# Moving half of an output block behind the last input products, and folding the last rows in two parts

## The chip, the core and the metric

The kernel runs on one core of one Trainium2 chip. The metric is the device time of one execution in microseconds (us); a comparison uses the median of several runs. TensorE (PE) does the matmuls, VectorE (DVE) and ScalarE (ACT) the elementwise work, GpSimd (POOL) and SyncE (SP) issue transfers here.

## What is computed

A backbone of two layers over 512 latent tokens of width 1024 and 256 context tokens. Layer 0 is a bidirectional retention mixer; layer 1, whose end the change concerns, is a chunked gMLP without context output:

```python
u = h @ w_in[:, :GM_WIDTH]                       # GM_WIDTH = 2048
v = (h @ w_in[:, GM_WIDTH:2 * GM_WIDTH])
z = h @ w_in[:, 2 * GM_WIDTH:]
...                                              # v is normalised
mixed = einsum('gij,bnjgc->bnigc', w_s, vg) + b_s
y = u * mixed
out = (y * silu(z)) @ w_out                      # 2048 -> 1024
x = x + gate_x * out
return rmsnorm(x, final_g)
```

All of it is float32. The kernel forms each float32 matmul as three matmuls on a high and a low half of both operands.

## The kernel before

**Operands.** `mm3` issues the three matmuls of a product. A weight block comes as a raw float32 tile of 128 x 1024, in two transfers of 256 KB; ScalarE casts it to the high half (a cast `hl<-raw`), and VectorE subtracts that from the raw to give the low half (`hl<-raw,hl`). The pairs lie in a ring of `HL = 4` tiles.

**Products.** A large product is done by Winograd's form of 2 x 2 blocks with seven block products instead of eight. A quad is the seven: B11, T1, T2, B21, T3, B22, T4 (`SINGLE`), each of 24 matmuls of 256 columns. The T blocks are differences of raw blocks, formed in place on VectorE (`raw<-raw`), so that a quad keeps its four raw tiles until T3, B22 and T4 have been split. ScalarE copies three of the banks out (`snap`), and VectorE adds three of them to other banks (`snap<-pst,snap`).

**The end of layer 1.** The loop `for i in range(UZ)` has eight quads (`UZ = 8`). Quad i gives u and z of two feature tiles, 2i and 2i + 1, for all 512 tokens. After B22 the mixing matmuls on v are issued (16 of 128 columns), then the gating `gate_f` of feature 2i + 1, then T4, then `gate_f` of 2i. `gate_f` runs on ScalarE and VectorE and splits the gated feature (`ya`) into the high and low half for the output product. The features lie in six places `ys[f % 6]`: four in `hc`, two in the tags `g2` and `g3` (`yb`).

After quads 2, 4 and 6 `out1(p)` multiplies four features (4p to 4p + 3) by `w_out`, for p = 0, 1, 2; `out1(3)` follows quad 7. A block p has two halves `hf` of 512 output columns, each with two weight tiles and, for each of four token tiles t, four features k: 12 matmuls of 512 columns into one PSUM bank. `out1(3)` takes in its first half the features k = 0, 1, 3 of all four token tiles first and k = 2 of all four after that. `drain` adds a bank to the running sum `o1[t]`; for p = 2 it also multiplies by the gate and adds the residual (`xs`, loaded from `x1_d`). For p = 3 `final` squares the row half with its sum on ScalarE, multiplies by the final weight, and, after the second half, scales the row: columns 0 to 511 on VectorE and 512 to 1023 on ScalarE, each stored by a transfer of its own.

**Order.** TensorE's queue is kept in the order of the text through the class `Queue`. Those of VectorE, ScalarE and SP are, in this part of the kernel, settled by a scheduler when the kernel is built. Each engine then works its queue in order. `Stream` (`Q`) holds the weight blocks in the order in which they are used and their loads in the same order. It has seven raw slots `w0` to `w6`; a load is issued by SP once a slot is free, that is, once its last block has been split. The blocks of `out1(3)` are multiplied by the layer's gate on VectorE before they are split (`raw<-raw,gateb`). `Q.get()` splits two blocks ahead of the one that it hands out. `add_out(p)` puts the four blocks of an output block into the list, at the place where `out1(p)` stands in the loop. PSUM has six banks for these products and two (`tm`) for other sums.

All calls on the engines go through line 54, so that the profile's lines say L54 and the groups are told by their tiles.

Of the kernel before, what the change touches and what calls it, by code (L numbers as in the profile page):

```python
# [8 lines left out]
F32R = mybir.dt.float32r  # L9
AF = mybir.ActivationFunctionType  # L10
ALU = mybir.AluOpType
AX = mybir.AxisListType

P = 128
D = 1024
KT = D // P
SEQ = 512
CTX = 256
HEADS = 4
NT = SEQ // P  # L20
# [6 lines left out]
HS = 256  # L27
# [40 lines left out]
def hybrid_kernel(ctx, tc, xT_d, cT_d, cv_d, sv_d, rows_d, ada0_d, adag_d, w_d, rope_d, dec_d, ws_d, id_d, out_d):  # L68
    nc = tc.nc
    pe, act, dve, sp = (Queue(tc, e) for e in (nc.tensor, nc.scalar, nc.vector, nc.sync))  # L70
# [11 lines left out]
    def st(shape, tag, dt=F32, bufs=1, name=None):  # L82
        return sb.tile(shape, dt, tag=tag, name=name or tag, bufs=bufs)

    T2 = 11
# [32 lines left out]
    def t2(name, shape=(P, 512), dt=F32):  # L118
        return st(list(shape), "t2", dt, bufs=T2, name=name)

    def pt(shape=(P, 512), tag="ps"):
        return ps.tile(list(shape), F32, tag=tag, name="pst", bufs=6 if tag == "ps" else 2)
# [3 lines left out]
    def mm3(out, l, r, first, last):  # L126
        (lh, ll), (rh, rl) = l, r
        mm(out, ll, rh, start=first, stop=False, skip_group_check=True)
        mm(out, lh, rl, start=False, stop=False, skip_group_check=True)
        mm(out, lh, rh, start=False, stop=last, skip_group_check=True)  # L130
# [13 lines left out]
    def load(dst, src):  # L144
        sp.dma_start(dst, src)
# [95 lines left out]
    def parts_of(q, u):  # L241
        kind, i = q[0], q[1]
        kh, nh = int(u[0]) - 1, int(u[1]) - 1
        if kind == "kq":
            b = 16 * i + (0 if nh else 2)
            return narrow_parts(b, b + 1, kh)
        if kind == "vz":
            return wide_parts(16 * i + (8 if nh else 4), kh, q[2])
        if kind == "v1":
            return wide_parts(64 + 4 * i, kh, nh)  # L250
        return narrow_parts(80 + 2 * i + nh, 96 + 2 * i + nh, kh)
# [30 lines left out]
            for cb in (a, b):  # L282
                Q.load((("v1", cb), u), V1_SLOTS, 2, parts_of(("v1", cb), u))

    def add_out(p):
        for j in range(4):
            q = ("o", 4 * p + j)
            h = j // 2 * 512
            Q.single(q, ("gated", h) if p == 3 else "plain")
            Q.load((q, "w"), W, 2, [(lambda r, e=e: r[:, 512 * e:512 * e + 512], w_d[112 + 4 * p + 2 * (j % 2) + e][:, h:h + 512])  # L290
                                    for e in range(2)])

    UZ = 8
    for i in range(UZ):
        Q.quad(("u", i), SINGLE)
        for u in RAWS:
            Q.load((("u", i), u), W, 2, parts_of(("u", i), u))
        if i and i % 2 == 0:
            add_out(i // 2 - 1)
    add_out(3)  # L300


# [269 lines left out]
    def project(q):  # L572
        if q[0] == "kq":
            return Product(features, kq_done(q[1]), hc)
        return Product(tokens, vz_done(q[1], q[2]), hc)
# [349 lines left out]
    for n, q in enumerate(QUADS[3:]):  # L925
        pr = project(q)
# [287 lines left out]
    fg = st([P, D], "g0", name="fg")  # L1214
# [9 lines left out]
    o1 = [st([P, D], f"s{t}", name="o1") for t in range(NT)]  # L1224
    ya = st([P, 4, 2, SEQ], "hc", F32R, name="ya")
    ys = [ya[:, i] for i in range(4)] + [st([P, 2, SEQ], f"g{i}", F32R, name="yb") for i in (2, 3)]

    def yf(f):
        return ys[f % 6]

    def out1(p):
        for hf in range(2):
            ws = [Q.get() for _ in range(2)]
            pr = {}
            if p == 3 and hf == 0:
                seq = [(t, k) for ks in ((0, 1, 3), (2,)) for t in range(NT) for k in ks]
            else:
                seq = [(t, k) for t in range(NT) for k in range(4)]
            ends = (2,) if p == 3 and hf == 0 else (3,)
            for t, k in seq:  # L1240
                if k == 0:
                    pr[t] = pt()
                y = yf(4 * p + k)
                w = ws[k // 2][:, :, k % 2 * 512:k % 2 * 512 + 512]
                mm3(pr[t], (y[:, 0, t * P:t * P + P], y[:, 1, t * P:t * P + P]), (w[:, 0, :], w[:, 1, :]), k == 0, k in ends)
                if k in ends:
                    drain(p, t, hf, pr.pop(t))

    def drain(p, t, hf, pr):
        h = slice(hf * 512, hf * 512 + 512)  # L1250
        s = o1[t][:, h]
        if p == 0:
            act.copy(s, pr)
            return
        dve.tensor_tensor(s, pr, s, ALU.add)
        if p == 2:
            xs = t2("xs")
            load(xs, x1_d[2 * t + hf])
            dve.tensor_tensor(s, s, Q.gate[:, h], ALU.mult)
            dve.tensor_tensor(s, s, xs, ALU.add)  # L1260
        if p == 3:
            final(t, hf, s, h)

    ends = {}

    def final(t, hf, s, h):
        if hf == 0:
            ends[t] = (st([P, 2], "fss", bufs=4), st([P, D], f"w{t}", name="o"))
        ss, o = ends[t]
        act.activation(t2("junk1"), s, AF.Square, accum_out=ss[:, hf:hf + 1])  # L1270
        if hf == 0:
            dve.tensor_scalar(ss[:, 0:1], ss[:, 0:1], 1.0 / D, EPS, ALU.mult, ALU.add)
        dve.tensor_tensor(o[:, h], s, fg[:, h], ALU.mult)
        if hf == 0:
            return
        rows = out_d[t * P:t * P + P, :]
        act.activation(ss[:, 1:2], ss[:, 1:2], AF.Sqrt, bias=ss[:, 0:1], scale=1.0 / D)
        dve.reciprocal(ss[:, 1:2], ss[:, 1:2])
        dve.tensor_scalar(o[:, 0:512], o[:, 0:512], ss[:, 1:2], None, ALU.mult)
        load(rows[:, 0:512], o[:, 0:512])  # L1280
        act.activation(o[:, 512:], o[:, 512:], AF.Copy, scale=ss[:, 1:2])
        load(rows[:, 512:], o[:, 512:])

    vts = {}

    def load_vt(i):
        vts[i] = []
        for th in range(2):
            v = t2("vt", (P, 2, HS))
            load(v, vt_d[i][:, 2 * th:2 * th + 2, :])  # L1290
            for t in range(2):
                n = 2 * th + t
                dve.tensor_scalar(v[:, t, :], v[:, t, :], mv[:, n, 0:1], rv[:, n:n + 1], ALU.subtract, ALU.mult)
            vts[i].append(v)

    def gate_f(f, pm, mine):

        g = f // 2
        a = t2("ya")
        z1 = t2("yz")  # L1300
        bb = bsb[:, g * P:g * P + P].unsqueeze(1).to_broadcast([P, NT, P])
        for th in range(2):
            act.activation(z1[:, th * HS:th * HS + HS], mine[th][:, HS:], AF.Silu)
        dve.scalar_tensor_tensor(a.rearrange("p (n i) -> p n i", n=NT), pm.rearrange("p (n i) -> p n i", n=NT),
                                 vg[:, f:f + 1], bb, ALU.mult, ALU.add)
        for th in range(2):
            h = a[:, th * HS:th * HS + HS]
            dve.tensor_tensor(h, mine[th][:, 0:HS], h, ALU.mult)
        dve.tensor_tensor(a, a, z1, ALU.mult)
        y = yf(f)  # L1310
        split((y[:, 0, :], y[:, 1, :]), a)

    load_vt(0)
    for i in range(UZ):
        got, pms = {}, {}
        prod = Product(features, got.__setitem__)
        for name in SINGLE:
            prod.run(name, Q.get())
            if name == "T2" and i < UZ - 1:
                load_vt(i + 1)  # L1320
            if name == "B22":
                for s in range(2):
                    pm = pms[s] = pt()
                    for n in range(NT):
                        mm(pm[:, n * P:n * P + P], vts[i][n // 2][:, n % 2, s * P:s * P + P], wsT[:, i * P:i * P + P], start=True, stop=True)
                gate_f(2 * i + 1, pms[1], {0: got["12"], 1: got["22"]})
        gate_f(2 * i, pms[0], {0: got["11"], 1: got["21"]})
        if i and i % 2 == 0:
            out1(i // 2 - 1)
    out1(3)  # L1330


# [108 lines left out]
```

## Time and profile before

| What | Value |
|---|---|
| Time, median of 3 runs | 906.26 us |
| The three runs | 908.04, 906.09, 906.26 us |
| Profiled execution: span from first to last instruction | 908.2 us |
| Profiled execution: its own time | not given apart from the span |
| Mean granted TensorE clock | 0.992 |
| VectorE's busy time | 720.0 us (79%) |
| Chain that ended last | PE 67%, DVE 19%, DMA 5%, ACT 4%, issue 4% |

The span is that of one execution, which isn't necessarily one of the three timed ones. A busy share is an average over stages. Times in the timeline are microseconds from the start of the span, and each row has its start, its duration, engine, operation, the tiles written and read, the count, and in brackets the idle time before it with what ended it. The granted clock is the share of TensorE's full speed that the throttle allowed in a window.

### The profile page before, as it was taken

The page shows a single profiled execution, that of the slowest core. Times are in us where ns is not written, and L with a number is a line of the kernel's source. Part 1 is how long each engine was busy: PE and PEld are TensorE (multiplying, and loading weights), DVE is VectorE, ACT ScalarE, POOL GpSimd, SP SyncE. Part 2 cuts the span into 40 slices and gives each one's busy share as a digit, 9 for nine tenths or more (in the row PEclk, how much of TensorE's full clock was granted, in tenths as well). Part 3 has the DMA queues.
Part 4 walks back from the last instruction along what each step waited for, and adds up shares of the span by engine and source line. Part 5 has one row for each costly group of instructions (what it writes and reads, how often), then busy time and mean ns, then how long its engine had stood idle before and what let it go on. Part 6 is the DMA issues. An engine that isn't in the chain of part 4 may idle for free.

```text
span 908.2 us, 16915 instructions
## 1 busy us (share of the span) xinstructions
PE 884.4 (97%) x6872; PEld 839.3 (92%) x6872; DVE 720.0 (79%) x1024; ACT 445.8 (49%) x683; POOL 51.4 (6%) x88
## 2 busy tenths in 40 slices
PE   8999999999999999999999999999999999999986
PEld 7899999999999999998989898999999899899875
DVE  3689967698689876888677669999899478689975
ACT  5564634434445435626263558654445444353334
POOL 0001201101101011000000001111000000000000
PEclk9999999999999999999999999999999999999999
DMA  9933957467477458758253611636335035128002
GB/s 338 399 121 109 320 194 255 153 191 223 154 237 239 140 183 316 255 161 260 79 184 118 209 47 59 215 96 211 118 117 187 24 116 187 44 96 283 19 24 93
DMA packets 76782, 153.81 MB, mean 169 GB/s; under 512 B 7840, under 2 KB 34592, under 8 KB 76704
## 3 DMA queue, kind: packets, MB, share of 16 engines
q1 hardware_dynamic: 69840, 130.70, 44.2%
q0 software_dynamic: 6720, 22.03, 6.4%
q8 instruction: 54, 0.88, 0.4%
q14 instruction: 24, 0.20, 0.1%
q10 hardware_dynamic: 144, 0.01, 0.0%
HBM read 128.58 MB, written 24.12 MB: 168 GB/s over the span
## 4 chain that ended last, share of the span: by engine, by line
PE 67%; DVE 19%; DMA 5%; ACT 4%; issue 4%; SPq 1%; DVEq 0%; ACTq 0%
PE pst L54 67%; DVE hl L54 6%; DMA raw<-in_w_dram 3%; DVE raw L54 3%; DVE ya L54 2%; DVE o L54 2%; DVE snap L54 1%; SPq L54 1%; DMA vt<-vt 1%; DMA xq<-in_xT_dram 1%; ACT hl L54 1%; DVE f L54 1%; DVE pf L54 1%; ACT junk L54 1%; DVE oS L54 1%
## 5 line engine op out<-in xcount | busy, mean ns | idle before, releaser
L54 DVE TENSOR_TENSOR hl<-raw,hl 128x1024 fp32r<-128x1024 f32 x195 | 236.0, 1219 | 68.0 <-ACT hl L54 67.8
L54 ACT CAST hl<-raw 128x1024 fp32r<-128x1024 f32 x195 | 203.7, 1050 | 129.0 <-PE pst L54 71.2
L54 PE MATMUL pst<-oS,hl 128*128 128x256 f32 x1104 | 135.6, 282 | 4.6 <-DVE hl L54 3.9
L54 PE MATMUL pst<-hl,oS 128*128 128x256 f32 x1152 | 137.8, 281 | 2.0 <-DVE hl L54 1.8
L54 PEld LDWEIGHTS pst<-hl,oS 128*128 128x128 f32 x1152 | 135.8, 190 | 3.5 <-DVE hl L54 2.3
L54 PEld LDWEIGHTS pst<-oS,hl 128*128 128x128 f32 x1104 | 131.4, 190 | 6.9 <-ACT ya L54 3.7
L54 PE MATMUL pst<-oA,hl 128*128 128x256 f32 x936 | 117.5, 281 | 0.7 <-DVE snap L54 0.5
L54 PEld LDWEIGHTS pst<-oA,hl 128*128 128x128 f32 x936 | 112.2, 189 | 3.2 <-issue 1.3
L54 DVE TENSOR_TENSOR raw<-raw 128x1024 f32<-128x1024 f32 x92 | 111.4, 1218 | 1.2 <-DMA raw<-in_w_dram 0.5
L54 ACT COPY snap<-pst 128x512 f32<-128x512 f32 x92 | 53.9, 586 | 103.4 <-PE pst L54 102.9
L54 PE MATMUL pst<-hl,oA 128*128 128x256 f32 x816 | 98.6, 279 | 0.4 <-DVE snap L54 0.4
L54 PEld LDWEIGHTS pst<-hl,oA 128*128 128x128 f32 x816 | 96.3, 189 | 0.6 <-issue 0.6
L54 PE MATMUL pst<-og,hl 128*128 128x256 f32 x768 | 92.5, 281 | 0.0
L54 PEld LDWEIGHTS pst<-og,hl 128*128 128x128 f32 x768 | 90.4, 189 | 0.9 <-DVE acc L54 0.2
L54 PE MATMUL pst<-hl,ya 128*128 128x512 f32 x288 | 70.8, 399 | 2.7 <-DVE ya L54 2.7
L54 PEld LDWEIGHTS pst<-hl,ya 128*128 128x128 f32 x288 | 54.9, 192 | 15.2 <-DVE ya L54 3.1
L54 PE MATMUL pst<-v,ph 128*128 128x512 f32 x192 | 60.1, 395 | 0.0
L54 DVE TENSOR_TENSOR snap<-pst,snap 128x512 f32<-128x512 f32 x69 | 47.2, 684 | 3.9 <-PE pst L54 3.6
L54 ACT CAST ph<-pf 128x512 fp32r<-128x512 f32 x24 | 14.9, 621 | 67.1 <-DVE pf L54 66.7
L54 PE MATMUL pst<-hl,hc 128*128 128x256 f32 x384 | 47.4, 280 | 0.0
L54 PEld LDWEIGHTS pst<-hl,hc 128*128 128x128 f32 x384 | 46.0, 189 | 0.0
L54 PEld LDWEIGHTS pst<-v,ph 128*128 128x128 f32 x192 | 36.2, 188 | 7.3
(171 smaller groups left out, 970.3 us busy)
## 6 DMA issues: line engine op xcount, KB each, us to landing
raw<-in_w_dram SPq DMA_DIRECT2D x224, 256.0 KB, 4.4
bg<-in_adag_dram SPq DMA_DIRECT2D x32, 512.0 KB, 4.3
ada_w<-in_ada_dram SPq DMA_DIRECT2D x16, 512.0 KB, 8.7
raw<-in_w_dram SPq DMA_DIRECT2D x16, 512.0 KB, 4.3
bg<-in_dec_dram SPq DMA_DIRECT2D x12, 512.0 KB, 4.4
v<-snap POOLq DMA_DIRECT2D x16, 256.0 KB, 5.0
z<-snap POOLq DMA_DIRECT2D x16, 256.0 KB, 4.2
v<-v SPq DMA_DIRECT2D x8, 512.0 KB, 4.3
```

The source lines that it names most:

```text
L54: made = op(*args, **kw)
```

## The change

Block 2 of the output product is taken apart: its first half stays behind quad 6, its second half comes behind quad 7, ahead of `out1(3)`. The list of the blocks and loads follows. The features of quad 7 (14 and 15) get places of their own, in the tag `oA11`, whose operand is last read by quad 7's B11; before, they lay in two of the six places. The special order of the first half of `out1(3)` is dropped: each token tile takes its features 0 to 3 in turn. The last token tile's second half is done in two parts of 256 columns, each with a bank of its own, by `last_part`: the first part is added, squared and multiplied by the final weight while the second is in the matmuls; the row is then scaled with columns 0 to 767 on VectorE and 768 to 1023 on ScalarE, and stored by one transfer of 512 KB.

```diff
-    def add_out(p):
-        for j in range(4):
+    def add_out(p, js=range(4)):
+        for j in js:
...
         if i and i % 2 == 0:
-            add_out(i // 2 - 1)
+            add_out(i // 2 - 1, range(4 if i < UZ - 2 else 2))
+    add_out(2, (2, 3))
     add_out(3)
...
+    late_y = []
+
     def yf(f):
-        return ys[f % 6]
+        return ys[f % 6] if f < 14 else late_y[f - 14]
 
-    def out1(p):
-        for hf in range(2):
+    def out1(p, hfs=range(2)):
+        for hf in hfs:
             ws = [Q.get() for _ in range(2)]
-            pr = {}
-            if p == 3 and hf == 0:
-                seq = [(t, k) for ks in ((0, 1, 3), (2,)) for t in range(NT) for k in ks]
-            else:
-                seq = [(t, k) for t in range(NT) for k in range(4)]
-            ends = (2,) if p == 3 and hf == 0 else (3,)
-            for t, k in seq:
-                if k == 0:
-                    pr[t] = pt()
...
+            for t in range(NT):
+                last = (p, hf, t) == (3, 1, NT - 1)
+                for c in range(2 if last else 1):
+                    n = HS if last else 512
+                    pr = pt((P, n))
+                    for k in range(4):
+                        y = yf(4 * p + k)
+                        w = ws[k // 2][:, :, k % 2 * 512 + c * n:k % 2 * 512 + c * n + n]
+                        mm3(pr, (y[:, 0, t * P:t * P + P], y[:, 1, t * P:t * P + P]), (w[:, 0, :], w[:, 1, :]), k == 0, k == 3)
+                    if last:
+                        last_part(t, c, pr)
+                    else:
+                        drain(p, t, hf, pr)
...
+    def last_part(t, c, pr):
+        ss, o = ends[t]
+        h = slice(512 + c * HS, 512 + c * HS + HS)
+        s = o1[t][:, h]
+        dve.tensor_tensor(s, pr, s, ALU.add)
+        act.activation(t2("junk1")[:, 0:HS], s, AF.Square, accum_out=ss[:, 1:2])
+        if c == 0:
+            dve.scalar_tensor_tensor(ss[:, 0:1], ss[:, 1:2], 1.0 / D, ss[:, 0:1], ALU.mult, ALU.add)
+        dve.tensor_tensor(o[:, h], s, fg[:, h], ALU.mult)
+        if c == 0:
+            return
+        rows = out_d[t * P:t * P + P, :]
+        act.activation(ss[:, 1:2], ss[:, 1:2], AF.Sqrt, bias=ss[:, 0:1], scale=1.0 / D)
+        dve.reciprocal(ss[:, 1:2], ss[:, 1:2])
+        act.activation(o[:, 768:], o[:, 768:], AF.Copy, scale=ss[:, 1:2])
+        dve.tensor_scalar(o[:, 0:768], o[:, 0:768], ss[:, 1:2], None, ALU.mult)
+        load(rows, o)
...
+            if name == "T2" and i == UZ - 1:
+                pair_y = st([P, 2, 2, SEQ], "oA11", F32R, name="yc")
+                late_y += [pair_y[:, j] for j in range(2)]
...
         if i and i % 2 == 0:
-            out1(i // 2 - 1)
+            out1(i // 2 - 1, range(2 if i < UZ - 2 else 1))
+    out1(2, (1,))
     out1(3)
```

More of the change, by code (lines that the diff above doesn't have):

```diff
@@ L1226, in hybrid_kernel @@
     ys = [ya[:, i] for i in range(4)] + [st([P, 2, SEQ], f"g{i}", F32R, name="yb") for i in (2, 3)]
+    late_y = []
     def yf(f):
-        return ys[f % 6]
-    def out1(p):
-        for hf in range(2):
+        return ys[f % 6] if f < 14 else late_y[f - 14]
+    def out1(p, hfs=range(2)):
+        for hf in hfs:
             ws = [Q.get() for _ in range(2)]
-            pr = {}
-            if p == 3 and hf == 0:
-                seq = [(t, k) for ks in ((0, 1, 3), (2,)) for t in range(NT) for k in ks]
-            else:
-                seq = [(t, k) for t in range(NT) for k in range(4)]
-            ends = (2,) if p == 3 and hf == 0 else (3,)
-            for t, k in seq:
-                if k == 0:
-                    pr[t] = pt()
[L1243 to L1247, printed above, removed]
+            for t in range(NT):
[11 more added lines that the diff above has]
+                        drain(p, t, hf, pr)
     def drain(p, t, hf, pr):
```

## The prediction

> **What bounds the kernel now.** I read the page first, then the windows and TensorE's own timeline over the last 80 us, then the other queues there.
>
> ```profile
> span 908.2 us, 16915 instructions
> PE 884.4 (97%) x6872; PEld 839.3 (92%) x6872; DVE 720.0 (79%) x1024; ACT 445.8 (49%) x683; POOL 51.4 (6%) x88
> ```
>
> TensorE is busy for 97% of the span, so an edit pays where TensorE stands still or runs slowly, or behind its last matmul. The change reaches nothing before 831 us. TensorE's timeline from there (start, duration, count, idle before):
>
> ```profile
> 831.13 1.55 PE L54 MATMUL pst<-hl,ya 128*128 128x512 f32 x6
> 842.11 1.54 PE L54 MATMUL pst<-hl,ya 128*128 128x512 f32 x6
> 853.07 2.99 PE L54 MATMUL pst<-oA,hl 128*128 128x256 f32 x24
> 855.90 5.82 PE L54 MATMUL pst<-oS,hl 128*128 128x256 f32 x48
> 871.75 3.07 PE L54 MATMUL pst<-oA,hl 128*128 128x256 f32 x24
> 874.66 1.56 PE L54 MATMUL pst<-hl,ya 128*128 128x512 f32 x6
> 878.93 22.47 PE L54 MATMUL pst<-hl,ya 128*128 128x512 f32 x90 [2.71 <-DVE ya L54]
> ```
>
> Output block 2 starts its halves at 831.13 and 842.11 and ends at 853.07: 96 matmuls in 21.94 us, 0.2285 each. The last quad, seven products of 24 matmuls (2.83 us each, 853.07 to 855.90) and the gating matmuls, fills 853.07 to 874.66 without a hole. Block 3 issues six matmuls, stops for 2.71 us until VectorE has gated the last features, and runs its other 90 in 22.47 us, where 90 x 0.2285 = 20.6 would do. The windows (after the span: PE, PEld, DVE, ACT, POOL busy; granted clock; DMA share; GB/s) show why:
>
> ```profile
> 876.20:878.90 2.70, 0.03 (x1) 0.00 (x0) 2.67 (x5) 1.15 (x2) 0.00 (x0) 1.00 0.00 0
> 880.00:881.00 1.00, 1.00 (x4) 0.79 (x3) 0.00 (x0) 0.00 (x0) 0.00 (x0) 0.60 0.00 0
> 881.00:882.00 1.00, 1.00 (x4) 0.78 (x3) 0.00 (x0) 0.00 (x0) 0.00 (x0) 0.50 0.00 0
> 882.00:883.00 1.00, 1.00 (x4) 0.81 (x3) 0.00 (x0) 0.00 (x0) 0.00 (x0) 0.50 0.00 0
> 883.00:884.00 1.00, 1.00 (x4) 0.76 (x4) 0.00 (x0) 0.00 (x0) 0.00 (x0) 0.69 0.00 0
> ```
>
> Behind the stop the granted clock falls to half for 3.4 us: 0.40 + 0.50 + 0.50 + 0.31 = 1.71 us of TensorE time lost. It happens after two other stops of this trace, and not after a shorter one:
>
> ```profile
> 224.03 4.50 PE L54 MATMUL pst<-hl,oS 128*128 128x256 f32 x23 [1.77 <-DVE hl L54]
> 660.60 4.48 PE L54 MATMUL pst<-oS,hl 128*128 128x256 f32 x24 [1.99 <-DVE hl L54]
> 749.44 2.98 PE L54 MATMUL pst<-oS,hl 128*128 128x256 f32 x24 [1.40 <-DVE hl L54]
> ```
>
> Products that take 2.98 us after a stop of 1.40 us take 4.5 us after stops of 1.77 and 1.99 us, so the stop at 876 us, longer than both, costs its own length and a slow stretch of about 1.7 us.
>
> **The move of the half block.** The same matmuls are issued; the second half of block 2 (842.11 to 853.07, 10.96 us) changes places with the quad. As both run without a hole, block 3 still starts at 874.66, provided the quad and the half find their operands in the new places. What goes is the stop: the last features are now gated while TensorE does the half. In the new instruction order VectorE's tightest step is T3's low half. Its pace:
>
> ```profile
> 845.04 1.22 DVE L54 TENSOR_TENSOR hl<-raw,hl 128x1024 fp32r<-128x1024 f32 x1
> 846.18 0.68 DVE L54 TENSOR_TENSOR o<-o,xs 128x512 f32<-128x512 f32 x1
> 846.78 1.22 DVE L54 TENSOR_TENSOR raw<-raw 128x1024 f32<-128x1024 f32 x1
> ```
>
> A 1024-wide operation takes 1.14 us of the queue, a 512-wide one 0.60. Up to 846.78 the new order has operations of the same sizes. Then come B21's low half, T3's and T4's subtractions, one gating of a raw block of block 3, and T3's low half: it starts at 846.78 + 4 x 1.14 = 851.34 and ends at 852.56. TensorE wants it at 842.11 + 4 x 2.83 = 853.43: 0.87 us in hand. B22's and T4's low halves follow at 1.14 us each and are wanted 2.83 us and more apart. The quad's weights were loaded before those of the moved half in either order, now earlier still.
>
> **The loads that are moved.** The quad keeps its four of the seven weight slots until T3, B22 and T4 are split, so block 3's last three raw blocks are issued by SP only then, the first at 852.56. The residual tiles of the moved half queue on SP behind these, and are wanted from the half's first drain on (863.7 + 12 x 0.2285 = 866.4). A wait is added: VectorE's gating of the first of those blocks stands in order ahead of the add that empties T3's bank, which T4's first matmul needs, and ahead of the moved half's second weights and the gate chain. The same kind of load in the trace, with the gating that waited for it:
>
> ```profile
> 864.41 0.80 SPq L54 DMA_DIRECT2D raw<-in_w_dram  x2
> 869.07 1.23 DVE L54 TENSOR_TENSOR raw<-raw,gateb 128x1024 f32<-128x1024 f32 x1
> ```
>
> 4.66 us, so the block is there at 857.2. VectorE arrives at 852.48 + 2 x 1.14 + 0.60 + 1.14 = 856.50 and waits 0.7 us. The add ends by 857.2 + 1.14 + 0.7 = 859.1; T4 is wanted at 871.75 - 10.96 = 860.79. Cost nothing, hidden by 1.7 us of TensorE's queue. Then the add (0.60), the low half, a gating, an add and a low half (3 x 1.14 + 0.60) bring VectorE to the gate chain at about 863.0:
>
> ```profile
> 873.08 1.40 DVE L54 SCALAR_TENSOR_TENSOR ya<-pst,sv,bsb 128x512 f32<-128x512 f32 x2
> 878.20 1.28 DVE L54 TENSOR_TENSOR ya<-ya 128x512 fp32r<-128x512 f32 x2
> ```
>
> The chain took 6.4 us; with one more gating of 1.14 in it the last feature is split at 863.0 + 7.5 = 870.5. Block 3 wants it at 874.66 + 6 x 0.2285 = 876.04: 5.5 us in hand. Then 8 drains of 0.60 and three waits for them (12 x 0.60) and two low halves end near 880; block 3's second half wants those at 885.6. The last features' own slot only lets them be written while block 2's are still read; by itself it costs nothing, since its old operand was read by B11.
>
> **The sum on TensorE.** Before, 874.66 to the end of the last matmul; after, 96 x 0.2285 = 21.94 us. The last group is 12 + 12 matmuls of 256 columns: 2.83 us a 24, against 12 x 0.2285 = 2.74, so 0.09 more.
>
> ```profile
> 900.78 0.62 PE L54 MATMUL pst<-hl,ya 128*128 128x512 f32 x2
> 901.44 0.69 DVE L54 TENSOR_TENSOR o<-pst,o 128x512 f32<-128x512 f32 x1
> 902.17 0.63 ACT L54 ACTIVATE junk<-o 128x512 f32<-128x512 f32 x1 [0.43 <-DVE o L54]
> 903.45 0.49 DVE L54 TENSOR_SCALAR o<-o,fss 128x512 f32<-128x512 f32 x1
> 903.96 0.33 SPq L54 DMA_DIRECT2D out_dram<-o  x1
> 904.38 0.38 SPq L54 DMA_DIRECT2D out_dram<-o  x1
> ```
>
> The last matmul ends at 901.40, 0.16 past its slot: 901.24 - 874.66 = 26.58 us before, 22.03 after, a gain of 4.55 (2.9 of standstill, 1.7 of slow clock, less 0.09).
>
> **The last rows.** The path from the last matmul to SP was 2.56 us. Its first two steps now work on 256 columns, its last on 768:
>
> ```profile
> L54 DVE TENSOR_TENSOR ya<-pst,ya 128x256 f32<-128x256 f32 x8 | 3.3, 416 | 0.0
> L54 ACT ACTIVATE yz<-snap 128x256 f32<-128x256 f32 x24 | 9.2, 414 | 29.5 <-DVE snap L54 29.5
> L54 DVE TENSOR_SCALAR ada_a<-bg,cpad 128x1024 f32<-128x1024 f32 x4 | 3.2, 803 | 0.0
> out_dram<-o SPq DMA_DIRECT2D x8, 256.0 KB, 2.3
> v<-v SPq DMA_DIRECT2D x8, 512.0 KB, 4.3
> ```
>
> The add falls from 0.69 to 0.42, the square from 0.63 to 0.41; the scaling rises from 0.49 to about 0.65 (midway to the 0.80 of 1024); VectorE, busy with the first part's folding, is some 0.05 late: 0.28 us gained. The first part's work lies beside the last 1.4 us of matmuls. One 512 KB transfer replaces two of 256 KB, issued 0.42 us apart. Below, it gains that 0.42; above, it lands like the 512 KB row, 4.3 against 0.42 + 2.3 from the first issue, 1.6 lost. I take 0: the same bytes leave from the same moment, which is nearest to the pair.
>
> Sum: 4.55 + 0.28 = 4.8 us; the profiled execution would go from 908.2 to 903.4. Its span lies 0.2 us above the slowest of the three timed runs (908.04) and 1.9 above their median, 906.26. That difference is the size of one slow stretch, so I read the two lower runs as having one less, out of the three seen. The stop at 876 us is the longest of the three, so the missing one is more likely one of the first two, which the change leaves alone. Then the gain holds from the median: 906.26 - 4.8 = **901.4 us**. Measured runs that have all the earlier slow stretches would lie at 908.04 - 4.8 = 903.2.
>
> **The rivals.** First, the slow stretch does not hang on this stop and stays somewhere in block 3, or was already absent in the median run: the gain is 4.8 - 1.7 = 3.1, and 903.2 us. For it: two timed runs lie a slow stretch lower. Against it: in this trace the halving follows each of the stops above 1.7 us. [...]
>
> Second, slower: the added wait decides. Where loads compete, this page has them much later:
>
> ```profile
> acc<-in_xT_dram SPq DMA_DIRECT2D x4, 512.0 KB, 11.8
> ```
>
> At 11.8 us the block lands at 864.4, T4 starts at 866.2 instead of 860.79, TensorE stands still for 5.4 us in the middle of the quad and pays 1.7 of slow clock: 7.1 - 4.8 = 2.3 lost, 908.6 us. It turns into a loss where the standstill exceeds 3.1 us, a landing 9.5 us after the issue. Against it: nothing but this load is under way then, and the like one took 4.66.
>
> **How the numbers follow.** Forecast 0.74, first rival 0.14, second 0.05, something I do not see 0.07 (mostly a shift of the 0.87 us margin that eats the gain). A change of 0.2%, 1.8 us, is about what can be told from none. Faster: 0.74 + 0.14 + 0.02 = 0.90; same 0.05; slower 0.05. The range reaches from 901.4 less 0.42 (the transfer) and 0.6 for the rounding of my steps, to 903.2 with half of the transfer's upper bound: 900.4 to 904.0.
>
> **What would show it.** Right: no idle TensorE from 831 us to the last matmul, clock 1.00 there, block 3 in about 22.0 us, the last features split near 870.5, one output transfer at the end. Wrong: idle TensorE ahead of T3 or T4 of the last quad, a clock below 1.00 in block 3 without a stop, or a longer stretch from the last matmul to the end than 908.2 - 901.40 = 6.8 us.

## The result, and the profile after

| Kernel | Median of 20 runs | Lowest to highest | Ratio to before, 95% interval |
|---|---|---|---|
| before | 906.26 us | 901.17 to 910.03 | |
| after | 901.33 us | 897.46 to 904.14 | 0.9941 [0.9928, 0.9953] |

The change gains 4.9 us; 901.4 was forecast. Of the profiled execution of after, both time and span are known:

```profile
span 895.7 us, 16947 instructions
PE 874.6 (98%) x6884; PEld 830.3 (93%) x6884; DVE 720.5 (80%) x1027; ACT 446.4 (50%) x685; POOL 51.6 (6%) x88
```

Its time is 897.46 us, 1.77 more than its span, which is 895.69 to two decimals. By the same offset the profiled execution of before (span 908.25) took about 910.0 us, nearly the longest of its 20 runs. The two spans differ by 12.6 us, and most of that is not the change: one profile lies near the top of its kernel's runs and the other at the bottom, and the runs spread by 7 to 9 us. So only the stretch from output block 2 on is compared, the stretch that the change rearranges. TensorE's timeline of after there (start, duration, count):

```profile
824.13 1.56 PE L54 MATMUL pst<-hl,ya 128*128 128x512 f32 x6
...
835.20 2.91 PE L54 MATMUL pst<-oA,hl 128*128 128x256 f32 x24
837.94 5.60 PE L54 MATMUL pst<-oS,hl 128*128 128x256 f32 x48
...
846.10 5.60 PE L54 MATMUL pst<-oS,hl 128*128 128x256 f32 x48
...
853.24 3.07 PE L54 MATMUL pst<-oA,hl 128*128 128x256 f32 x24
856.15 1.56 PE L54 MATMUL pst<-hl,ya 128*128 128x512 f32 x6
...
867.22 1.54 PE L54 MATMUL pst<-hl,ya 128*128 128x512 f32 x6
868.59 1.54 PE L54 MATMUL pst<-hl,yc 128*128 128x512 f32 x6
...
888.48 0.84 PE L54 MATMUL pst<-hl,yc 128*128 128x256 f32 x6
```

No row from 824.13 on carries an idle time. Block 2's first half runs 824.13 to 835.20, the last quad to 856.15, the moved half to 867.22, block 3 to 889.32. The windows there (PE, PEld, DVE, ACT, POOL busy; granted clock; DMA share; GB/s) have the clock at 1.00:

```profile
861.00:871.00 10.00, 10.00 (x45) 8.20 (x44) 9.93 (x15) 2.21 (x3) 0.00 (x0) 1.00 0.00 0
871.00:881.00 10.00, 10.00 (x46) 8.19 (x45) 6.77 (x14) 2.90 (x8) 0.00 (x0) 1.00 0.01 2
881.00:889.00 8.00, 8.00 (x48) 7.01 (x47) 5.89 (x14) 6.01 (x15) 0.00 (x0) 1.00 0.30 115
```

From block 2's start to the end of the span it is 908.25 - 831.13 = 77.12 us before and 895.69 - 824.13 = 71.56 us after, 5.6 less in these two profiles. Four terms make it up: the stop (2.71) and its slow stretch (1.71); the quad, 21.59 us before and 20.95 after (0.64); and the end behind the last matmul, 908.25 - 901.40 = 6.85 before and 895.69 - 889.32 = 6.37 after (0.48).

VectorE has the step that was expected to be tight. From its timeline in after:

```profile
843.55 3.49 DVE L54 TENSOR_TENSOR hl<-raw,hl 128x1024 fp32r<-128x1024 f32 x3
...
849.04 1.23 DVE L54 TENSOR_TENSOR raw<-raw,gateb 128x1024 f32<-128x1024 f32 x1 [0.27 <-DMA raw<-in_w_dram]
850.18 0.68 DVE L54 TENSOR_TENSOR snap<-pst,snap 128x512 f32<-128x512 f32 x1
...
861.51 0.68 DVE L54 TENSOR_TENSOR yc<-ya,yc 128x512 fp32r<-128x512 f32 x1
```

T3's low half is the first of the three from 843.55 and is done at 844.77; T3's matmuls begin with the row at 846.10: 1.3 us in hand. The new wait for a moved load is in the row at 849.04: 0.27 us. The last feature's low half ends at 862.19 and is wanted at 868.59.

### The profile page after: what moved, and what is told of

Its sections match the earlier page's. It is cut to its first block, busy times and chain, and to the rows that moved or that the text cites. A ratio compares the mean times of both kernels' runs of the same rounds, so it can differ in the third digit from the quotient of the medians.

```text
span 895.7 us, 16947 instructions
## 1 busy us (share of the span) xinstructions
PE 874.6 (98%) x6884; PEld 830.3 (93%) x6884; DVE 720.5 (80%) x1027; ACT 446.4 (50%) x685; POOL 51.6 (6%) x88
## 4 chain that ended last, share of the span: by engine, by line
PE 70%; DVE 17%; ACT 5%; DMA 4%; issue 3%; SPq 1%; DVEq 0%; ACTq 0%
PE pst L54 70%; DVE hl L54 6%; DVE raw L54 3%; DMA raw<-in_w_dram 2%; DVE ya L54 2%; ACT hl L54 1%; DMA xq<-in_xT_dram 1%; DVE snap L54 1%; DMA vt<-vt 1%; DVE f L54 1%; DVE pf L54 1%; ACT junk L54 1%; SPq L54 1%; DVE oS L54 1%; ACT f L54 1%
## 5 line engine op out<-in xcount | busy, mean ns | idle before, releaser
L54 PE MATMUL pst<-hl,oS 128*128 128x256 f32 x1152 | 134.0, 277 | 2.1 <-DVE hl L54 1.9
L54 PEld LDWEIGHTS pst<-hl,oS 128*128 128x128 f32 x1152 | 132.0, 188 | 3.6 <-DVE hl L54 2.4
L54 PE MATMUL pst<-hl,ya 128*128 128x512 f32 (+1 forms) x246 | 59.6, 388 | 0.0
L54 PEld LDWEIGHTS pst<-hl,ya 128*128 128x128 f32 x246 | 45.4, 188 | 9.8
```

The lines of the kernel that those rows point to most:

```text
L54: made = op(*args, **kw)
```

## The experiments

The theory is the prediction's: the gain is the stop and the slow clock behind it, both gone because other matmuls cover the gating. The rivals are that the slow clock does not hang on this stop, and that something else in the change (the last rows, the place of the quad) brings the gain. e1 to e4 ran on one chip, beside 34 runs of before (906.84 us), and e5 to e8 on another, beside 17 (906.45). Beside the profiles stands each kernel's granted clock averaged over all its runs; one slow stretch in a run lowers that by 1.71 / 907 = 0.0019. The average also holds the very end of a run: in after's profile the clock falls to half at 892.63, 3.3 us behind the last matmul, which costs nothing and makes the mean 0.998 all the same. So only kernels with an end of the same length are compared by it.

| Kernel | Median, us | Ratio to before, 95% | Clock, mean over runs | Block 2's start to end of span, us |
|---|---|---|---|---|
| before | 906.84, 906.45 | | 0.9958, 0.9956 | 77.12 |
| after, 20 runs | 901.33 | 0.9941 [0.9928, 0.9953] | 0.9972 | 71.56 |
| e1, stop filled, 22 matmuls | 907.27 | 0.9998 [0.9980, 1.0016] | 0.9973 | 78.15 |
| e5, stop filled, 11 matmuls | 905.01 | 0.9989 [0.9973, 1.0005] | 0.9971 | 75.43 |
| e2, no places of their own | 909.17 | 1.0021 [1.0003, 1.0038] | 0.9941 | 80.03 |
| e4, last rows alone | 905.84 | 0.9988 [0.9970, 1.0005] | 0.9963 | 77.31 |
| e3, move with plain last rows | 900.66 | 0.9934 [0.9914, 0.9954] | 0.9979 | 72.02 |
| e8, the same again | 900.93 | 0.9932 [0.9915, 0.9950] | 0.9975 | 71.51 |
| e7, after again | 901.23 | 0.9932 [0.9914, 0.9950] | 0.9967 | 71.56 |
| e6, early stops filled too | 901.60 | 0.9934 [0.9917, 0.9950] | 0.9985 | 71.54 |

**The stop filled (e1).** The order of before, with matmuls on constants whose result nobody reads in the place of the stop:

```diff
             for t, k in seq:
...
+                if (p, hf, t, k) == (3, 0, 0, 3):
+                    keep_on = pt(tag="tm")
+                    for i in range(22):
+                        mm(keep_on[:, :P], ones, ones, start=True, stop=True, skip_group_check=True)
```

> The kernel before, with 22 matmuls of 128 columns on a constant, whose result nobody reads, issued in the stop of block 3 (each 0.11 us, 2.5 us in all, behind its sixth matmul). The stop stays, only TensorE does not idle in it. Theory (the idle time halves the clock): no clock below 1.00 in block 3, its 96 matmuls and the stop end 1.7 us earlier after the start of output block 2 (span end at 75.4 us after it, against 77.07), median about 1.4 to 1.7 us under the kernel before in the runs that had the slow stretch there, near 904.8. First rival (the slow stretch does not hang on this stop): clock at half in block 3 as before, 77.1 us, median unchanged near 906.3.

Measured: no gain, 0.9998 [0.9980, 1.0016]. TensorE's timeline of e1 says why:

```profile
872.08 1.57 PE L54 MATMUL pst<-hl,ya 128*128 128x512 f32 x6
873.48 5.07 PE L54 MATMUL pst<-ones 128*128 128x128 f32 x44
878.31 20.85 PE L54 MATMUL pst<-hl,ya 128*128 128x512 f32 x90
```

The 22 instructions are 44 records and last 4.83 us, not 2.7: the filler ran some 2 us past the stop and ate what the clock gave. The 90 matmuls behind it take 20.85 us where before took 22.47: 1.62 less, so in this profile the slow clock is gone. The filler was sized wrongly, so that the times tell nothing of the gain. The experiment was made again with half the filler.

**The stop filled, shorter (e5).** The same edit with `range(11)`.

> The kernel before with 11 instead of 22 idle matmuls in the stop of block 3: in the first try each took 0.22 us and not 0.11, so that the 22 ran on for 1.9 us after the features were ready. Eleven take 2.4 us, inside the stop. Theory: block 3 at full clock, its last 90 matmuls in 20.8 us against 22.5, mean clock over the runs as in the first try (0.9972 against 0.9958 of the kernel before), median 1.2 to 1.7 us under the kernel before. Rival (the slow stretch costs nothing in the end, or lies elsewhere): median as the kernel before.

From TensorE's timeline of e5 and its windows:

```profile
871.15 2.62 PE L54 MATMUL pst<-ones 128*128 128x128 f32 x22
874.00 20.88 PE L54 MATMUL pst<-hl,ya 128*128 128x512 f32 x90 [0.23 <-DVE ya L54]
```

```profile
876.00:879.00 3.00, 3.00 (x15) 2.46 (x14) 0.00 (x0) 0.00 (x0) 0.00 (x0) 1.00 0.02 5
879.00:881.00 2.00, 2.00 (x11) 1.63 (x10) 0.00 (x0) 0.00 (x0) 0.00 (x0) 1.00 0.00 0
```

Block 3 begins as late as before, but the 90 matmuls take 20.88 us at clock 1.00. The median falls by 1.4 us; its interval includes no change, so the times alone do not settle it. The clock over all runs does better: 0.9956 and 0.9958 before, 0.9971 and 0.9973 with the stop filled. The difference, 0.0014 x 906 = 1.3 us a run, is 0.7 of a slow stretch (the standard error of each of the two differences, from the spread of the runs' clocks, is 0.0005 to 0.0006). So the slow clock does hang on this stop, which the first rival denied, but by this estimate it is there in some 7 of 10 runs and not in each.

**Without the features' own places (e2).** After, with features 14 and 15 in the ring of six:

```diff
-        return ys[f % 6] if f < 14 else late_y[f - 14]
+        return ys[f % 6]
...
-            if name == "T2" and i == UZ - 1:
-                pair_y = st([P, 2, 2, SEQ], "oA11", F32R, name="yc")
-                late_y += [pair_y[:, j] for j in range(2)]
```

> The kernel after, with the last two features in the places of the ring (f % 6) instead of their own slot. Theory (the slot only lets them be written while block 2 still reads those places, and without it nothing is hidden): they are split only behind the moved half, TensorE stops for about 2.5 us in block 3 behind its sixth matmul, with the slow stretch behind it in most runs; span end about 76.5 us after the start of output block 2, median near 906. Rival (the move of the half alone makes the gain): no stop, 71.6 us, median near 901.3.

In this text the gating of quad 7 stands ahead of the moved half, so the half multiplies features 14 and 15 where it should have 8 and 9. TensorE's timeline of e2, and a window:

```profile
857.08 3.07 PE L54 MATMUL pst<-oA,hl 128*128 128x256 f32 x24
866.54 2.93 PE L54 MATMUL pst<-hl,ya 128*128 128x512 f32 x6 [6.39 <-DVE ya L54]
```

```profile
866.00:868.00 2.00, 1.46 (x4) 1.17 (x5) 0.49 (x1) 0.00 (x0) 0.00 (x0) 0.50 0.00 0
```

A stop was expected, but a shorter one and behind the half; it is 6.39 us and ahead of it, since the half itself now waits for the gating, and the clock is at half behind it. The whole gate chain stands open. From block 2's start to the end it takes 80.03 us, where 76.5 was expected and the rival had 71.6, and the gain becomes a small loss, 1.0021 [1.0003, 1.0038]. So without places of their own for the last features the moved half covers nothing. What the places cost or gain in the order of before was not tried.

**The last rows alone (e4).** Before, with only `last_part` for the last token tile of block 3's second half:

```diff
+            if p == 3 and hf == 1:
+                seq = [(t, k) for t, k in seq if t < NT - 1]
...
+            if p == 3 and hf == 1:
+                t = NT - 1
+                for c in range(2):
+                    bank = pt((P, HS))
+                    for k in range(4):
...
+                    last_part(t, c, bank)
```

> The kernel before with only the last token tile's second half in two parts of 256 columns and one transfer. Theory: stop and slow stretch of block 3 as in the kernel before; from the last matmul's end to the span's end 6.4 us against 6.8, median 0.3 us under the kernel before, near 906.0, not to be told from it. Rival (the last rows are a large part of the gain): 2 us or more under it.

Measured 0.9988 [0.9970, 1.0005]: 1.0 us at the medians, not told from nothing. Its TensorE timeline keeps the stop and the slow clock of before:

```profile
876.44 22.75 PE L54 MATMUL pst<-hl,ya 128*128 128x512 f32 x102 [2.59 <-DVE ya L54]
```

From the last matmul to the end it takes 6.12 us, where 6.4 was expected and the order of before takes 6.85 (in e1 and e5 too): here the two parts do shorten the end, by 0.7.

**The move with plain last rows (e3, and e8 once more).** After, with `last` never true, so that the last token tile is one group of 512 columns with two transfers:

```diff
-                last = (p, hf, t) == (3, 1, NT - 1)
+                last = False
```

> The kernel after, with the last token tile's second half in one part of 512 columns, folded and stored in two transfers as in the kernel before. Theory: from the last matmul's end to the span's end 6.8 us as in the kernel before, against 6.38 after, and TensorE 0.09 us shorter: 0.3 us slower than after, median 901.6, within the noise of the times. Rival (the last rows are a large part of the gain, by the transfer saved): 7.5 us or more behind the last matmul, median 902.5 or more.

> The kernel after with the last rows in one part, once more beside after. Theory of the prediction: 0.3 us above after. Rival (the two parts bring nothing, since the first part's scaling on ScalarE stands ahead of the second part's square): as after or below it.

Measured 0.9934 [0.9914, 0.9954] and 0.9932 [0.9915, 0.9950], beside after's 0.9941 and 0.9932: the move alone has the whole gain, and in the new order the two parts bring nothing that can be measured. The end behind the last matmul takes 6.27 and 6.28 us with plain rows, not the 6.8 that was expected, and 6.37, 6.37 and 6.34 with two parts (after, e7, e6).

**After again (e7), and the early stops filled (e6).** e7 is after, unchanged, for a ratio to the same runs of before. e6 was meant to beat both: after, with 6, 3 and 3 unread matmuls ahead of T2 of three earlier quads, where the profiles have stops of up to 2 us.

```diff
+            if name == "T2":
+                n_fill = FILL.get(t2_calls[0], 0)
+                t2_calls[0] += 1
+                if n_fill:
+                    self.y = pt(tag="tm")
+                    for i in range(n_fill):
+                        mm(self.y[:, :P], ones, ones, start=True, stop=True, skip_group_check=True)
```

> The kernel after once more, beside the others on one chip: 0.994 of the kernel before, mean clock 0.997.

> The kernel after with idle matmuls in three stops that it shares with the kernel before: 6 (1.3 us) ahead of T2 of the eighth projection quad (stop of 1.77 to 1.94 us near 223 us) and 3 each (0.7 us) ahead of T2 of quads 1 and 2 of u and z (0.7 to 2.0 us near 659 and 682 us). Theory (stops this long halve the clock by chance, and shorter ones don't): no slow stretch behind these places, mean clock over the runs 0.999 against 0.9972 after, 0.8 to 1.5 us under after, near 900. Rival (the idle matmuls delay what comes behind them as much as the clock gains): median as after or above, 901.3 or more.

From TensorE's timeline of e6:

```profile
222.03 1.50 PE L54 MATMUL pst<-ones 128*128 128x128 f32 x12
...
224.08 2.89 PE L54 MATMUL pst<-hl,oS 128*128 128x256 f32 x23 [0.43 <-DVE hl L54]
...
657.81 3.06 PE L54 MATMUL pst<-oS,hl 128*128 128x256 f32 x24 [0.35 <-DVE hl L54]
...
681.67 2.98 PE L54 MATMUL pst<-oS,hl 128*128 128x256 f32 x24 [1.37 <-DVE hl L54]
```

The stops behind the filler are 0.4 to 1.4 us and the mean clock is the highest of all, 0.9985. But a filled stop still ends when the operand is there, and the time, 901.60, is no better than 901.23. By the clock 0.0013 to 0.0018 x 901 = 1.2 to 1.6 us a run was to be had against after; the six runs of each kernel spread over 2.6 and 4.3 us and do not show it. So no version here beats after by what these runs can tell.

## Why the prediction was right, point by point

| Step | Predicted | Measured |
|---|---|---|
| Standstill removed, less the narrower matmuls | 2.9 - 0.09 | 2.7 in the profile; none left |
| Slow clock removed | 1.7 | 1.7 in the profile; 1.3 as an average over runs |
| Quad's TensorE time | unchanged | 0.64 less in the profile; not shown to come from the move |
| Last rows | 0.28 | 0.48 in the profile, but 0.57 without the two parts |
| From block 2's start to the end | 4.8 less | 5.6 less in the profile |
| The median | 4.8 less | 4.9 less |

**The move, right.** Block 3 takes 22.10 us where 22.0 was expected. To compare the other steps, 7.00 us is added to after's times, by which its block 2 starts earlier. T3's low half is done at 851.77 (852.56 predicted) and wanted at 853.10 (853.43). The moved load lands in 4.25 us (4.66), VectorE waits 0.27 (0.7), and the add that T4 needs is done at 857.86 (859.1). The last feature is split at 869.19 (870.5) and wanted at 875.59 (876.04). The second rival would have needed a landing of over 9.5 us; later loads than these were not tried. The change also drops the special order of block 3's first half, and that was not tried by itself either.

**The slow clock, right in kind and too sure.** The argument was that each stop of 1.77 us or more halves the clock. After has stops of that length with no loss behind them:

```profile
220.47 2.89 PE L54 MATMUL pst<-hl,oS 128*128 128x256 f32 x23 [1.94 <-DVE hl L54]
677.60 2.98 PE L54 MATMUL pst<-oS,hl 128*128 128x256 f32 x24 [1.78 <-DVE hl L54]
```

The first is the product that took 4.50 us in before; it takes 2.89 here. The second is the same product of a later quad than the one that took 4.48 us, and takes 2.98. Over the profiles of before, after and the experiments except e6, 4 of 11 stops between 1.7 and 2.0 us were followed by a slow clock, and all three longer ones (2.59, 2.71 and 6.39 us). What tells them apart was not shown. At the stop that the change removes it comes to 0.7 of a stretch per run, estimated from the clocks of e1 and e5. The first rival's case, the stretch absent, is therefore part of the runs rather than a case of its own.

**The quad, put at nothing, differed.** In the order of before T3 can be late, as TensorE's timeline of e1 shows (e4 has 0.58 at the same place):

```profile
861.92 5.70 PE L54 MATMUL pst<-oS,hl 128*128 128x256 f32 x48 [0.59 <-DVE hl L54]
```

In the four profiles of that order (before, e1, e4, e5) the quad takes 21.59, 22.10, 22.17 and 21.32 us; in the five of the moved order (after, e3, e6, e7, e8) 20.95, 21.58, 20.95, 20.96 and 20.96, with no wait. The means differ by 0.7 us. Part of it is T3's wait, part the rhythm told of below: e3, which runs the quad in the slow rhythm throughout, takes as long as before, so that the 0.64 between the profiles of before and after is not shown to come from the move. The quad's place was not tried by itself.

**The last rows, wrong in size.** 0.28 us was counted because the path's first steps shrink. ScalarE's and VectorE's timelines of after:

```profile
888.97 0.71 ACT L54 ACTIVATE o<-o,fss 128x512 f32<-128x512 f32 x1
...
890.23 0.42 ACT L54 ACTIVATE junk<-o 128x256 f32<-128x256 f32 x1 [0.55 <-ACT o L54]
```

```profile
889.45 0.41 DVE L54 TENSOR_TENSOR o<-pst,o 128x256 f32<-128x256 f32 x1
...
891.29 0.62 DVE L54 TENSOR_SCALAR o<-o,fss 128x768 f32<-128x768 f32 x1
```

The add did fall to 0.41 and ends at 889.86, but the square starts 0.37 later, where in before it started 0.04 behind the add (902.13 to 902.17). The row puts the wait down to ScalarE's scaling of the row before. But that ended at 889.68, ahead of the add, and in e4 the same scaling stands ahead and the square starts 0.09 behind the add, as ScalarE's and VectorE's timelines of e4 show:

```profile
898.87 0.71 ACT L54 ACTIVATE o<-o,fss 128x512 f32<-128x512 f32 x1
899.85 0.42 ACT L54 ACTIVATE junk<-o 128x256 f32<-128x256 f32 x1 [0.27 <-DVE o L54]
```

```profile
899.35 0.41 DVE L54 TENSOR_TENSOR o<-pst,o 128x256 f32<-128x256 f32 x1
```

So what holds the square back in after is open. The stores, from SP's timelines of after and of e3:

```profile
891.98 0.33 SPq L54 DMA_DIRECT2D out_dram<-o  x1
```

```profile
898.00 0.81 SPq L54 DMA_DIRECT2D out_dram<-o  x2
```

After's one store is issued 2.65 us behind the last matmul instead of 2.56 - 0.28 = 2.28 (e4: 2.41), and the span ends 3.72 later; the plain pair in e3 is issued at 2.56 and 2.98, and the span ends 3.3 after the second. So the single transfer, taken at nothing, costs about what the pair does, and the sum of the last rows is 0 or a little less (6.34 to 6.37 against 6.27 and 6.28). That the end is 0.5 shorter than before comes with the moved order, plain rows or not. The plain pair is issued at the same 2.56 and 2.98 in before, where the span ends 3.87 behind the second, so what is gained lies in the landing; why is open.

**The reading of the span, wrong and harmless.** The prediction set the span (908.2) against the run times as if they were the same thing and read the median run as one slow stretch shorter. With 1.77 us between span and time the profiled run lay 3.7 above the median. The result held because the sum was a difference within one stretch of the trace. Errors cancel in it: the average run saves less on the clock (1.3 for 1.7) and on the last rows (0 for 0.28), and more in the quad and at the end (about 0.7 and 0.5). So 4.8 against 4.9 is closer than the working earned: the mechanism was right, the closeness is in part luck.

## What to carry to other kernels

A stop that waits for a short chain on another engine is worth its length and often a slow clock behind it, here after 4 of 11 stops of 1.7 to 2.0 us and after all three longer ones (2.59, 2.71 and 6.39 us); cover it with work whose operands have long been there, and give the results of the chain places of their own, or the covering work waits for the same chain. Compare two profiles only over the stretch that an edit rearranges, from an anchor that both have, and take a run's distance from the median into account before reading their spans. A shorter step on a final path need not shorten the path: here the next step began later behind it, and only the end of the last store tells what was gained.

## What the runs showed of the hardware

**The length of a stop alone does not tell whether the clock falls behind it.** A trace records when the granted clock changes. In that of before the three slow stretches begin at 224.85, 661.75 and 880.21 us, 436.9 and 218.5 us apart, and each lasts 3.4 us at clock 0.50. Over all the profiles there are seven ahead of the last matmul: three in before, one each in e2 and e3, two in e4. One product, near 223 us, waits 1.94 us in seven of the profiles. TensorE's timelines of e3, e4, e7 and e8 there, one row of each in this order:

```profile
223.45 4.32 PE L54 MATMUL pst<-hl,oS 128*128 128x256 f32 x23 [1.94 <-DVE hl L54]
223.18 4.33 PE L54 MATMUL pst<-hl,oS 128*128 128x256 f32 x23 [1.94 <-DVE hl L54]
223.21 2.89 PE L54 MATMUL pst<-hl,oS 128*128 128x256 f32 x23 [1.94 <-DVE hl L54]
223.68 2.88 PE L54 MATMUL pst<-hl,oS 128*128 128x256 f32 x23 [1.94 <-DVE hl L54]
```

In after, e2 and e5 it takes 2.89, 2.88 and 2.89 us. Behind a stop of 1.77 us the same product takes 4.50 us in before and 2.90 in e1. So the shortest stop with a slow clock behind it is 1.77 us and the longest without one 1.94. What else decides was not shown.

**The same product runs in two rhythms.** 24 matmuls of 256 columns take 2.83 us in one and 2.74 in the other: after's quad goes from 835.20 to 837.94, before's from 853.07 to 855.90, both without idle time at clock 1.00. In the traces successive matmuls start 117 to 119 ns apart or 113 to 114, one rhythm holds for up to 911 matmuls (59.81 to 168.76 us in before's), and it changes at stops and between forms: at 750.1 us in before's, behind the stop of 1.40 us, and at 835.8 in after's, with the first product of the last quad. Of some 5500 such distances 42% are of the quick kind in before's profile, 64% in after's, and 33 to 41% in the other runs. At 4.5 ns each, the 0.23 between after's profile and e7's (40%) is 5.7 us of TensorE's work. The page of e7:

```profile
span 896.5 us, 16947 instructions
PE 879.8 (98%) x6884; PEld 836.5 (93%) x6884; DVE 721.0 (80%) x1027; ACT 446.2 (50%) x685; POOL 51.5 (6%) x88
```

TensorE is busy 5.2 us longer than in after's profile, but the span is only 0.8 longer: where its matmuls are quicker, TensorE is idle longer, 21.1 us of the span in after's profile against 16.7 in e7's. What sets the rhythm, and how much of the spread of 7 to 9 us among the runs of a kernel is due to it, is open.
